# A convolution of 31 taps moved in part to TensorE: three channel groups as products of two taps each, one group on VectorE

## The chip, the cores and the metric

The kernel runs on one core of a Trainium2 chip. The metric is the device time of one execution in microseconds. TensorE multiplies matrices into PSUM, VectorE, ScalarE and GpSimd work on elements, SyncE issues most DMAs. Each engine takes its own instructions in order, and waits at the head of its queue when an operand is not ready.

## What is computed

Two layers of a streaming encoder on 256 tokens of 1024 channels: SwiGLU, mixer, SwiGLU in each, with RMS norms around. Layer 0 has the recurrent mixer that the change touches. Half of it is a delta-rule recurrence with 8 heads of 64 (computed here in four chunks of 64 tokens), the other half a causal convolution over 512 channels with 31 taps per channel, followed by a layer norm and SiLU:

```python
glu = c_val * jax.nn.sigmoid(c_gate)
conv = lax.conv_general_dilated(
    glu, conv_w[:, None, :], window_strides=(1,), padding=[(CONV_WIDTH - 1, 0)],
    dimension_numbers=('NWC', 'WIO', 'NWC'), feature_group_count=D_CONV) + conv_b
y_b = jax.nn.silu(layer_norm(conv, conv_ln_g, conv_ln_b, CONV_LN_EPS))
return jnp.concatenate([y_a, y_b], axis=-1) @ w_out
```

The layer norm needs all 512 channels of a token, and `w_out` needs both halves. All values are float32.

## The kernel before

Weights come as pages of 128 x 1024 floats (512 KB) into ten load buffers, in the order of use, on SP's queue. `Stream.page` then splits a page into a rounded part `whi` (ScalarE) and a rest `wlo` (VectorE, for some pages GpSimd), and a load can start when the page ten places earlier has been split. The large products use the two parts in three passes; the small products of the mixer take plain float32, which TensorE runs as two rows (two passes) each.

`mixer_a` calls its pieces in the order of `ORDER`; a scheduler then orders each engine's queue by a simulated timeline, so neighbouring pieces mix. The ones that matter here:

- `invert` (I) sends 64x64 matrices through memory and inverts their 16x16 blocks on VectorE; the results land in `G` and `T`.
- `glu` (C) makes the gated input of the convolution, channels on partitions in four groups of 128, tokens along the free axis.
- `conv` (c) sets the taps up. Groups 0 and 1 are VectorE's (60 taps, one multiply-add each, handed out by `feed`). Group 2 has 24 taps on TensorE, each a product with a diagonal matrix `dw` that ScalarE makes from the tap (handed out by `pfeed`), and six taps with group 3's thirty on ScalarE (multiply) and GpSimd (add).
- `amats` (A) makes the attention matrices `ak` and `ar` of the four chunks: TensorE products into two PSUM banks, four VectorE evictions per chunk. It hands out taps and products after each chunk.
- `doubling` (2) grows the inverses from 16 to 64: ten groups of 16 small products (`each`), 64x64 in one corner of the array, each group followed by a pair of convolution products, each evicted by VectorE (`WT`, `G`, `T`) and followed by taps.
- `convend` (n) adds up the rest and runs `conv_norm` for both token halves; `state` (S) is the recurrence over four chunks (`R,G`, then `vz`, `vz,kb`, `vz,ar`, `SB`), and `outproj` multiplies by `w_out`, convolution half first. The next SwiGLU follows.

The small products use four PSUM banks in turn (`abank`), group 2's sum one of the two `gu` banks.

## Time and profile before

| | us |
|---|---|
| median of three runs (1122.34 to 1145.09) | 1124.52 |
| profiled execution | 1123.03 |
| its span on the core | 1121.2 |
| mean granted TensorE clock | 0.983 |
| TensorE busy (share of the span) | 1075.6 (96%) |
| VectorE busy | 668.3 (60%) |
| ScalarE busy | 568.5 (51%) |
| GpSimd busy | 255.1 (23%) |

The profile is one execution, times in us from the start of the span. A matmul row's duration holds its way through the array, so the distance between the starts of neighbouring rows, not their duration, is what a row costs in a stream. Float32 products appear as two rows each. A name like `acc<-T,Q` is output and inputs, buffer numbers left out. The granted clock is given as a share of 2.4 GHz: 1.00 is 2.4 and 0.50 is 1.2 GHz, and values between are a mean over a stretch at either level.

### The profile page before, as it was taken

What the parts mean: (1) busy time and instruction counts of PE and PEld (TensorE: products, weight loads), DVE (VectorE), ACT (ScalarE), POOL (GpSimd) and SP (SyncE); (2) the same over time, 40 slices, a digit from 0 to 9 for tenths busy, and PEclk for the clock granted to TensorE, in tenths of its full rate; (3) what the DMA queues carried; (4) which work ended last, traced back from release to release, by engine and by line L of the source; (5) the groups of instructions that cost most, each with busy time, mean ns of one, the idle gap of its engine ahead of it and who ended that gap; (6) DMA issues with size and microseconds to landing.
All of it is one profiled execution on the core that took longest, in us unless ns stands there. A gap on an engine that the chain in (4) does not pass through costs nothing.

```text
span 1121.2 us, 17652 instructions
## 1 busy us (share of the span) xinstructions
PE 1075.6 (96%) x6955; PEld 947.1 (84%) x6955; DVE 668.3 (60%) x1064; ACT 568.5 (51%) x933; POOL 255.1 (23%) x194
## 2 busy tenths in 40 slices
PE   7999999999698899999989999999999989999997
PEld 5899998889587789999878999988887868999986
DVE  4465661599887556547444555836667665555722
ACT  7444553673453464446354544634666945444611
POOL 4200006571662170000070000001564540000000
PEclk9999999998798999999999999999999999999999
DMA  9766785245410246557554464744273553765400
GB/s 361 246 212 185 235 308 177 86 165 151 104 39 1 76 151 244 201 189 271 168 186 151 167 227 170 240 138 151 90 286 107 193 189 101 226 193 179 148 1 37
DMA packets 65321, 189.27 MB, mean 169 GB/s; under 512 B 18360, under 2 KB 19672, under 8 KB 65238
## 3 DMA queue, kind: packets, MB, share of 16 engines
q1 hardware_dynamic: 55386, 186.18, 49.4%
q10 hardware_dynamic: 9852, 1.96, 1.0%
q8 instruction: 54, 0.88, 0.3%
q14 instruction: 29, 0.24, 0.1%
HBM read 184.68 MB, written 2.92 MB: 167 GB/s over the span
## 4 chain that ended last, share of the span: by engine, by line
PE 66%; DVE 7%; ACT 2%; DMA 1%; issue 1%; POOL 1%; ACTq 0%; DVEq 0%; POOLq 0%
PE gu L352 23%; PE acc L263 16%; PE gu L223 12%; PE gu L338 5%; PE acc L370 3%; PE gu L585 2%; PE acc L585 2%; DVE cv L926 2%; DVE wlo L99 1%; DVE x L148 1%; PE tr L158 1%; POOL p L484 1%; PE tr L506 1%; ACT whi L98 0%; DMA raw<-in_cout_dram 0%
## 5 line engine op out<-in xcount | busy, mean ns | idle before, releaser
L98 ACT CAST whi<-raw 128x1024 fp32r<-128x1024 f32 x294 | 303.4, 1047 | 206.2 <-PE gu L352 110.8
L99 DVE TENSOR_TENSOR wlo<-raw,whi 128x1024 fp32r<-128x1024 f32 x248 | 312.5, 1266 | 133.9 <-ACT whi L98 108.1
L352 PE MATMUL gu<-xth,wlo 128*128 128x256 f32 x1104 | 314.1, 284 | 0.0
L352 PE MATMUL gu<-xl,whi 128*128 128x256 f32 x1104 | 313.1, 284 | 0.0
L352 PE MATMUL gu<-xth,whi 128*128 128x256 f32 x1104 | 313.1, 284 | 0.0
L352 PEld LDWEIGHTS gu<-xth,wlo 128*128 128x128 f32 x1104 | 212.0, 192 | 3.5 <-issue 0.9
L352 PEld LDWEIGHTS gu<-xth,whi 128*128 128x128 f32 x1104 | 211.8, 192 | 3.3 <-issue 0.7
L352 PEld LDWEIGHTS gu<-xl,whi 128*128 128x128 f32 x1104 | 211.9, 192 | 1.0 <-issue 0.8
L99 POOL TENSOR_TENSOR wlo<-raw,whi 128x1024 fp32r<-128x1024 f32 x46 | 113.9, 2506 | 300.1 <-PE gu L223 141.5
L263 PE MATMUL acc<-whi,ht 128*128 128x512 f32 x576 | 168.0, 393 | 0.0
L113 POOL TENSOR_TENSOR misc<-misc 128x1 f32<-128x1 f32 (+1 forms) x36 | 31.6, 880 | 476.0 <-DVE misc L130 380.7
L263 PEld LDWEIGHTS acc<-whi,ht 128*128 128x128 f32 x576 | 104.0, 189 | 18.3
L263 PE MATMUL acc<-wlo,ht 128*128 128x512 f32 x288 | 89.9, 392 | 0.0
L234 DVE TENSOR_TENSOR h<-gu,h 128x256 f32<-128x256 f32 x88 | 36.9, 420 | 77.9 <-ACT h L230 74.7
L232 DVE TENSOR_TENSOR h<-gu,misc 128x256 f32<-128x256 f32 x56 | 23.7, 424 | 80.1 <-PE gu L352 80.1
L223 PE MATMUL gu<-whi,xth 128*128 128x512 f32 x160 | 63.8, 403 | 1.8 <-ACT whi L98 1.8
L223 PE MATMUL gu<-wlo,xth 128*128 128x512 f32 x160 | 64.0, 400 | 0.5 <-DVE wlo L99 0.5
L263 PEld LDWEIGHTS acc<-wlo,ht 128*128 128x128 f32 x288 | 53.9, 188 | 11.8
L223 PE MATMUL gu<-whi,xl 128*128 128x512 f32 x160 | 63.3, 400 | 0.1
L233 ACT ACTIVATE h<-h 128x256 f32<-128x256 f32 x56 | 23.2, 415 | 53.7 <-DVE h L232 53.7
L230 ACT ACTIVATE h<-gu,misc 128x256 f32<-128x256 f32 x32 | 15.1, 475 | 66.9 <-PE gu L223 36.9
L338 PE MATMUL gu<-whi,xth 128*128 128x512 f32 x112 | 44.9, 401 | 1.1 <-ACT xth L162 0.9
(254 smaller groups left out, 1589.6 us busy)
## 6 DMA issues: line engine op xcount, KB each, us to landing
raw<-in_wgc_dram SPq DMA_DIRECT2D x112, 512.0 KB, 4.5
raw<-in_wd_dram SPq DMA_DIRECT2D x88, 512.0 KB, 4.7
raw<-in_wgt_dram SPq DMA_DIRECT2D x64, 512.0 KB, 5.3
raw<-in_cin_dram SPq DMA_DIRECT2D x24, 512.0 KB, 5.2
raw<-in_ain_dram SPq DMA_DIRECT2D x18, 512.0 KB, 4.5
raw<-in_aout_dram SPq DMA_DIRECT2D x8, 512.0 KB, 5.1
raw<-in_cgate_dram SPq DMA_DIRECT2D x8, 512.0 KB, 7.5
raw<-in_cout_dram SPq DMA_DIRECT2D x8, 512.0 KB, 3.7
```

The lines of the kernel that those rows point to most:

```text
L98: self.nc.scalar.copy(out=hi, in_=raw)
L99: (engine or self.nc.vector).tensor_tensor(out=lo, in0=raw, in1=hi.bitcast(F32), op=ALU.subtract)
L113: self.pow = self.nc.gpsimd.tensor_tensor(out=out, in0=v, in1=self.mhalf[:, :n], op=ALU.pow)
L223: nc.tensor.matmul(ps, lhsT=l, rhs=r[:, k % 2], start=n == 0, stop=n == 23)
L232: nc.vector.tensor_tensor(out=z, in0=ps[:, 0:256], in1=self.rb, op=ALU.mult)
L233: nc.scalar.activation(sl, z, AF.Silu)
L234: nc.vector.tensor_tensor(out=h, in0=ps[:, 256:512], in1=sl, op=ALU.mult)
L263: mm = nc.tensor.matmul(out, lhsT=l, rhs=r, start=u[1] == 0 and i + n == 0, stop=u[1] == NB - 1 and i * 3 + n == 5)
L338: self.nc.tensor.matmul(ps, lhsT=l, rhs=r[:, k % 2], start=n == 0, stop=n == 23)
L352: self.nc.tensor.matmul(ps[:, j * 256:(j + 1) * 256], lhsT=l, rhs=r, start=n == 0, stop=n == 23)
L370: self.nc.tensor.matmul(accs[t][c], lhsT=l, rhs=r[:, 0, c * 512:(c + 1) * 512], start=k == ks[0] and n == 0, stop=k == ks[7] and n == 2)
L585: return nc.tensor.matmul(out, lhsT=lhsT, rhs=rhs, start=start, stop=stop, skip_group_check=True)
```

## The change

Group 0 stays on VectorE (30 taps). Groups 1 to 3 go to TensorE as six blocks of 64 channels (`j` = 2 to 7), eight products each: the moving operand has 64 channels on one partition half and the same channels one token late on the other half (`gl[0]`, `gl[1]`; SP copies from half to half, four DMAs), so that a product with an offset of 2s tokens covers two taps. The columns of the weight make two sums, of which the second holds the taps that lie 16 tokens back; ScalarE takes the first sum with the bias into one partition half, VectorE copies the second, 16 tokens on, into the other, and a product with two stacked identities (`twice`) in `conv_norm` adds them as it transposes. The weights are six new pages `acw` that come ready from memory and are used from their load buffers without a split. The sums live in one of the four banks of `abank`, which has three while `busy`. The taps and products are handed out in other numbers (`FEED`, `PFEED`), the last 20 products behind `R,G` in chunks 0 and 1 of `state`, and `convend` now runs in chunk 1 behind its products. In `qmats`, `amats` and `each` the small products stand in another order: partition halves in turn, where before one half came whole.

```diff
-ORDER = "VLDKPQkRIBCcbA2nS"
+ORDER = "VLDKPQkRIBCcbA2S"
-CSPLIT, PTAPS = 6, 24
-FEED, PFEED = (4, 3, 12), (1, 2)
+FEED, PFEED = (3, 2, 6), (2, 2, 10)
...
             i, cols, _, pooled, early, whole = pg
             self.load(i + 1 + self.ahead)
             raw = self.tiles[i]
+            if whole:
+                pg[2] = raw.rearrange("p (k f) -> p k f", f=cols)
+                return pg[2]
...
+        def abank():
+            return self.abank(3 if m.get("busy") else 4)
...
         def qmats():
...
-                for hp in range(2):
+                for g in range(4):
                     for c in range(2):
-                        for g in range(4):
+                        for hp in range(2):
...
         def amats():
...
-                for hp in range(2):
-                    for g in range(4):
+                for g in range(4):
+                    for hp in range(2):
                         b = slice(64 * hp, 64 * hp + 64)
                         i = mm(pss[hp][:, g, :], both(bk, g, t, c)[b], both(ur, g, t, c)[b])
...
         def glu():
...
+            gl = m["glu"] = [grp(self.page("glu")) for _ in range(2)]
+            own, late = (slice(0, 64), slice(64, P)), (slice(64, P), slice(0, 64))
...
-                V.tensor_tensor(out=gl[:, 2 * h:2 * h + 2, :], in0=cv[:, 2 * h:2 * h + 2, :], in1=z, op=ALU.mult)
+                gs = slice(max(2 * h, 1), 2 * h + 2)
+                if h == 0:
+                    V.tensor_tensor(out=gl[0][:, 0, :], in0=cv[:, 0, :], in1=z[:, 0, :], op=ALU.mult)
+                for i, (o, l) in enumerate(zip(own, late)):
+                    m["gated"] = V.tensor_tensor(out=gl[i][o, gs, :], in0=cv[o, gs, :], in1=z[o, gs.start - 2 * h:2], op=ALU.mult)
+                    nc.sync.dma_start(out=gl[i][l, gs, 1:256], in_=gl[i][o, gs, 0:255])
...
             def each(t, lhsT, rhs):
...
-                for c in range(2):
-                    for h in range(8):
+                for h in range(8):
+                    for c in range(2):
                         cs = slice(64 * c, 64 * c + 64)
                         i = mm(ps[cs, h, :], lhsT(cs, h), rhs(cs, h))
                 pfeed(PFEED[1], i)
...
         def conv():
...
-                    elif g == 2 and 31 - CSPLIT - PTAPS <= d < 31 - CSPLIT:
-                            nc.scalar.activation(dw[:, i % 8, :], self.ident, AF.Copy, scale=w)
...
-                    elif g == 3 or g == 2 and d > 31 - CSPLIT:
-                        nc.scalar.activation(z, gl[:, g, 0:256 - d], AF.Copy, scale=w)
-                        nc.gpsimd.tensor_tensor(out=o, in0=z, in1=o, op=ALU.add)
...
+            W.upto(("acw",))
+            m["pconv"] = self.bank("acc11").rearrange("p (i t) -> p i t", t=256)
+            m["busy"] = True
+            m["ptaps"] = ((j, s, w[:, s, :]) for j, w in enumerate(W.get(("acw",)), 2) for s in range(8))
+            nc.gpsimd.memset(m["cval"][64:P, :, 0:16], 0.0)
+            nc.scalar.activation(m["cv"][0], m["glu"][0][:, 0, :], AF.Identity, scale=par("cw", 30), bias=par("cb0"))
+            m["taps"] = iter(range(1, 31))
...
         def pfeed(n, behind=None):
...
-                    mm(m["pconv"][:, d:256], w, m["glu"][:, 2, 0:256 - d], d == 31 - CSPLIT - PTAPS, d == 30 - CSPLIT)
+                    mm(o[:, 2 * s:256], w, m["glu"][j % 2][:, j // 2, 0:256 - 2 * s], s == 0, s == 7)
+                if s == 7:
+                    z = m["cv"][j]
+                    nc.scalar.activation(z[0:64], o[0:64], AF.Identity, bias=par("cb", j)[0:64])
+                    V.tensor_copy(out=z[64:P, 16:256], in_=o[64:P, 0:240])
...
         def conv_norm(t):
...
-            for g in range(4):
-                nc.tensor.transpose(out=tp[:, g * P:(g + 1) * P], in_=cv[:, g, t * P:(t + 1) * P], identity=self.ident)
+            nc.tensor.transpose(out=tp[:, 0:P], in_=m["cv"][0][:, ts], identity=self.ident)
+            for j in range(2, 8):
+                mm(tp[:, 64 * j:64 * j + 64], m["cv"][j][:, ts], self.twice)
...
         def state():
...
                 V.tensor_tensor(out=h8(vz[t][zs, c, :]), in0=pz[zs], in1=m["nn"][zs, t, :].unsqueeze(2).broadcast_to([64, 8, 64]), op=ALU.mult)
+                pfeed(PFEED[2], i)
...
+                if ch == 1:
+                    convend()
```

The first place is TensorE's queue at the start of the doubling. Before, `glu,dw` are group 2's products, `T,Q` the first groups, `vz,ak` part of chunk 0 of the recurrence:

```order
L585 MATMUL acc_3093<-ur,bk 128x128 x4
L585 MATMUL gu<-glu,dw 128x255
L585 MATMUL gu<-glu,dw 128x254
L585 MATMUL gu<-glu,dw 128x253
L585 MATMUL gu<-glu,dw 128x252
L585 MATMUL gu<-vz,ak 64x64 x8
L585 MATMUL acc_3112<-T,Q 64x64 x16
L585 MATMUL gu<-glu,dw 128x251
L585 MATMUL gu<-glu,dw 128x250
L585 MATMUL acc_3135<-T,Q 64x64 x16
L585 MATMUL gu<-glu,dw 128x249
L585 MATMUL gu<-glu,dw 128x248
```

And after, where `glu,raw` are the products of the six blocks (`raw` is the load buffer):

```order
L590 MATMUL acc_3061<-ur,bk 128x128 x4
L590 MATMUL gu<-vz,ak 64x64 x4
L590 MATMUL acc_3062<-ur,bk 128x128 x4
L590 MATMUL acc_2987<-glu,raw 128x244
L590 MATMUL acc_2987<-glu,raw 128x242
L590 MATMUL acc_3083<-T,Q 64x64 x16
L590 MATMUL acc_3105<-T,Q 64x64 x14
L590 MATMUL acc_2987<-glu,raw 128x256
L590 MATMUL acc_2987<-glu,raw 128x254
L590 MATMUL acc_3105<-T,Q 64x64 x2
L590 MATMUL acc_2987<-glu,raw 128x252
L590 MATMUL acc_2987<-glu,raw 128x250
```

The products ahead of the first group were four with made weights and are now eight with loaded ones, in pairs between the blocks of `amats`; four more stand behind the second group. The first group stands behind all of `amats` in both. Within a group the text of the rows is the same: the order of halves shows in the code alone.

The second place is VectorE's queue at the same time. `z` is the second half of the gate, `glu<-cv,z` the gate products, `ak` and `ar` the evictions of `amats`, `cv<-glu,cst,cv` the taps. Before:

```order
L773 COPY inv<-inv 128x256
L845 TENSOR_TENSOR z<-gu,misc 128x512
L847 TENSOR_TENSOR glu<-cv,z 128x512
L818 TENSOR_TENSOR ak<-acc_3035,cst 64x4x64
L821 TENSOR_TENSOR ar<-acc_3035,cst 128x4x64
L818 TENSOR_TENSOR ak<-acc_3036,cst 64x4x64
L821 TENSOR_TENSOR ar<-acc_3036,cst 128x4x64
L926 SCALAR_TENSOR_TENSOR cv<-glu,cst,cv 128x255 x2
L818 TENSOR_TENSOR ak<-acc_3054,cst 64x4x64
L821 TENSOR_TENSOR ar<-acc_3054,cst 128x4x64
L926 SCALAR_TENSOR_TENSOR cv<-glu,cst,cv 128x254 x2
L845 TENSOR_TENSOR z<-gu,misc 128x512
```

And after, where the taps are `glu<-glu,cst`:

```order
L866 TENSOR_TENSOR glu<-cv,z 64x256 x2
L778 COPY inv<-inv 128x256
L858 TENSOR_TENSOR z<-gu,misc 128x512
L823 TENSOR_TENSOR ak<-acc_3004,cst 64x4x64
L826 TENSOR_TENSOR ar<-acc_3004,cst 128x4x64
L823 TENSOR_TENSOR ak<-acc_3005,cst 64x4x64
L826 TENSOR_TENSOR ar<-acc_3005,cst 128x4x64
L930 SCALAR_TENSOR_TENSOR glu<-glu,cst 128x255
L866 TENSOR_TENSOR glu<-cv,z 64x512 x2
L823 TENSOR_TENSOR ak<-acc_3023,cst 64x4x64
L826 TENSOR_TENSOR ar<-acc_3023,cst 128x4x64
L930 SCALAR_TENSOR_TENSOR glu<-glu,cst 128x254
```

The second `z` stood behind four taps and six evictions, and now stands ahead of all; taps come singly.

The third place is SP's queue, with the copies from half to half (`glu<-glu`), the next stage's weights (`in_wgt`) and the inverses (`G`, `T`). Before:

```order
L69 DMA raw<-in_wgt_dram 128x1024
L740 DMA dq<-Q 64x8x64 x2
L69 DMA raw<-in_wgt_dram 128x1024 x4
L104 DMA gp<-in_gpost_dram 128x1024
L69 DMA raw<-in_wgt_dram 128x1024
L778 DMA G<-dg 64x8x64 x2
L778 DMA T<-dt 64x8x64 x2
```

And after:

```order
L106 DMA ln<-in_arow_dram 128x1024
L68 DMA raw<-in_acw_dram 128x1024 x3
L68 DMA raw<-in_wgt_dram 128x1024
L867 DMA glu<-glu 64x255 x2
L783 DMA G<-dg 64x8x64 x2
L783 DMA T<-dt 64x8x64 x2
L867 DMA glu<-glu 64x2x255 x2
L68 DMA raw<-in_wgt_dram 128x1024 x4
```

The first two copies stand behind one weight load of the next stage, the other two behind `G` and `T`; seven of the next stage's eight first pages are now behind them.

## Rows read from the trace of the kernel before

**Rows 1.** Busy time by stretch: length, TensorE, weight loads, VectorE, ScalarE, GpSimd, clock, DMA share, GB/s.

```profile
286.87:304.17 17.30, 6.52 (x65) 6.09 (x65) 14.29 (x23) 9.57 (x19) 12.76 (x7) 0.69 0.67 131
304.17:314.15 9.98, 9.94 (x96) 8.12 (x96) 5.60 (x16) 8.99 (x26) 4.04 (x7) 0.85 0.01 2
314.15:340.35 26.20, 23.80 (x304) 20.58 (x305) 25.27 (x42) 13.54 (x28) 19.16 (x28) 1.00 0.15 42
340.35:359.00 18.65, 16.95 (x184) 13.92 (x183) 14.06 (x31) 5.75 (x10) 3.75 (x5) 0.82 0.00 1
359.00:393.99 34.99, 32.11 (x192) 26.12 (x191) 19.83 (x35) 15.87 (x31) 5.62 (x5) 0.95 0.18 61
```

**Rows 2.** TensorE's timeline: start, duration, operation, rows; in brackets idle time and releaser.

```profile
304.17 3.45 PE L585 MATMUL gu<-glu,dw 128*128 128x255 f32 x8 [8.51 <-ACT dw L906]
...
314.89 1.90 PE L585 MATMUL acc<-G,WT 64*64 64x64 f32 x32 [0.78 <-DVE WT L866]
316.72 1.10 PE L585 MATMUL gu<-glu,dw 128*128 128x247 f32 x4
317.75 1.90 PE L585 MATMUL acc<-WT,G 64*64 64x64 f32 x32
319.57 1.09 PE L585 MATMUL gu<-glu,dw 128*128 128x245 f32 x4
```

**Rows 3.** VectorE's timeline: evictions, taps, gate.

```profile
292.29 2.65 DVE L926 SCALAR_TENSOR_TENSOR cv<-glu,cst,cv 128x255 f32<-128x255 f32 x2
294.97 0.43 DVE L818 TENSOR_TENSOR ak<-acc,cst 64x256 f32<-64x256 f32 x1
...
295.75 4.15 DVE L926 SCALAR_TENSOR_TENSOR cv<-glu,cst,cv 128x254 f32<-128x254 f32 x2
299.83 0.68 DVE L845 TENSOR_TENSOR z<-gu,misc 128x512 f32<-128x512 f32 x1
...
303.33 0.69 DVE L847 TENSOR_TENSOR glu<-cv,z 128x512 f32<-128x512 f32 x1
303.94 0.87 DVE L926 SCALAR_TENSOR_TENSOR cv<-glu,cst,cv 128x252 f32<-128x252 f32 x2
...
314.15 1.29 DVE L866 TENSOR_TENSOR WT<-acc,cst 128x512 f32<-128x512 f32 x2 [4.34 <-PE gu L585]
```

**Rows 4.** GpSimd's timeline at the same time.

```profile
290.44 2.81 POOL L99 TENSOR_TENSOR wlo<-raw,whi 128x1024 fp32r<-128x1024 f32 x1
293.21 1.45 POOL L889 TENSOR_TENSOR gg<-ln,gg 128x512 f32<-128x512 f32 x1
294.62 5.00 POOL L99 TENSOR_TENSOR wlo<-raw,whi 128x1024 fp32r<-128x1024 f32 x2
```

**Rows 5.** TensorE's timeline in chunk 1 of the recurrence.

```profile
352.20 0.69 PE L585 MATMUL acc<-vz,kb 128*64 128x64 f32 x16 [0.79 <-DVE vz L988]
352.72 1.10 PE L585 MATMUL gu<-vz,ar 128*64 128x64 f32 x16
353.75 0.66 PE L951 MATMUL tr<-cst,xc 128*128 128x128 f32 x4
```

**Rows 6.** TensorE's timeline behind the output product.

```profile
393.99 0.39 PE L223 MATMUL gu<-whi,xl 128*128 128x512 f32 x1
```

**Rows 7.** Busy time by stretch, two shorter ones, columns as in rows 1.

```profile
304.17:307.60 3.43, 3.43 (x9) 2.54 (x9) 3.38 (x10) 3.43 (x12) 0.00 (x0) 0.55 0.02 5
340.35:349.00 8.65, 7.96 (x66) 6.37 (x65) 8.03 (x18) 1.17 (x2) 1.03 (x2) 0.61 0.00 0
```

**Rows 8.** DMA issues of the stretch 200 to 300: queue, count, KB, us to landing.

```profile
prev<-pv ACTq DMA_DIRECT2D x2, 30.0 KB, 2.3
```

**Rows 9.** VectorE's timeline: first statistics and first split of the normalised half.

```profile
349.10 0.70 DVE L940 BATCH_NORM_STATS2 misc<-tr 128x6 f32<-128x512 f32 x1 [0.62 <-PE tr L938]
...
358.55 0.69 DVE L99 TENSOR_TENSOR xl<-yb,xth 128x512 fp32r<-128x512 f32 x1 [1.52 <-ACT xth L98]
```

More of the change, by code (lines that the diff above doesn't have):

```diff
@@ L53, in __init__, with add @@
         self.where, self.pages = {}, []
-    def add(self, key, ap, cols):
+    def add(self, key, ap, cols, whole=False):
         self.where.setdefault(key, [])
@@ L918, in conv @@
-            m["taps"], m["ptaps"] = iter(taps), iter(ptaps)
-            m["pconv"] = self.bank("gu", 2)[:, 0:256]
+            W.upto(("acw",))
+            m["pconv"] = self.bank("acc11").rearrange("p (i t) -> p i t", t=256)
+            m["busy"] = True
+            gl = m["glu"]
+            m["cv"] = [gl[1][:, 0, :], None] + [m["cval"][:, i, :] for i in range(4)] + [gl[i][:, 1, :] for i in range(2)]
+            m["ptaps"] = ((j, s, w[:, s, :]) for j, w in enumerate(W.get(("acw",)), 2) for s in range(8))
@@ L960, in convend @@
             pfeed(99)
-            for d, z in ((31 - CSPLIT - PTAPS, m["pconv"]), (31 - CSPLIT, m["part"])):
-                o = m["cv"][:, 2, d:256]
-                V.tensor_tensor(out=o, in0=z[:, d:256], in1=o, op=ALU.add)
+            m["busy"] = False
             for t in range(2):
@@ L970, in state @@
             ak, ar, kb, vz, ur, pc, G, Gg, Wg = (m[z] for z in ("ak", "ar", "kb", "vz", "ur", "pc", "G", "gg", "Wg"))
-            R = half(self.page("R"))
+            R = m["Q"].rearrange("p t h x -> p t (h x)")
             SB = self.temp("SB", [4, P])
@@ L1065, in plan @@
                     W.add(("ao", h // 2), flat(a["aout"][h]), 1024)
+                for j in range(6):
+                    W.add(("acw",), flat(a["acw"][j]), 128, True)
             if st == "C":
```

93 lines of the change are left out of this document (45 added, 48 removed).

## The prediction

> **What bounds the kernel now.** I read the page first for where the mixer lies, then the chain of waits for which engine holds it, then the busy time by stretch, then each engine's timeline there. The order of the built programs is the same on all engines outside the mixer and the first units of the stage behind it, so only 286.87 to 393.99 us is costed; the rest keeps its time.
>
> [rows 1] cuts that into five stretches. In the first (attention matrices, 17.30 us) TensorE works 6.52 us: it is not the bound. [rows 2] names its one long wait: 8.51 us until 304.17, for `dw`, the diagonal matrices that ScalarE makes of the taps, held behind the second gate. That gate's VectorE part `z` stands at 299.83, behind two taps of 4.15 us [rows 3]. In the third stretch (block doubling, 26.20 us) TensorE is busy 23.80 and VectorE 25.27: two bounds at once. There [rows 2] shows a steady beat: a group of 32 rows (16 products of 64x64, two rows each) takes 317.75 to 319.57 = 1.82 us, a pair of convolution products (four rows) 316.72 to 317.75 = 1.03. In the fourth TensorE has 1.70 us idle but a granted clock of 0.82, in the fifth 2.88 us idle.
>
> **Part 1, up to the first doubled block** (`WT`, 314.15 in [rows 3]). The wait for `dw` goes: the weights now come from memory, and the order puts both `z` ahead of all evictions. TensorE has there, ahead of the first group's end, its old 6.52 us [rows 1], eight products of 0.515 and blocks of some 2 us, 12.6 together, which fits. What sets the end is VectorE's queue, which has from 286.87 on: one `z` 0.68, two gate products of 0.69, 16 evictions of 0.43, 11 taps and one copy of about half a pair, 0.43 each [rows 3]. That is 0.68 + 1.38 + 6.88 + 5.2 = 14.1 us: the first `WT` at 301.0. This is the lower end. The upper end comes from GpSimd. [rows 4] shows it busy from 290.44 to 299.62, and [rows 3] what a tap costs then: the pair at 292.29 ends when the GpSimd rows of 290.44 and 293.21 have ended, the pair at 295.75 when both weight splits have, 2.65 and 4.15 us against 0.87 for the pair at 303.94. The evictions, which read a bank of PSUM, stay at 0.43. If each VectorE instruction with both inputs in SBUF costs one GpSimd row, then by 299.6 there have passed the gate products, the copy of the inverse, one tap and four evictions; 12 evictions, 10 taps and a copy remain, 5.2 + 4.3 + 0.4 = 9.9, and `WT` starts at 309.5. I take 307.0, near the hindered end, since both hindered pairs are two to five times the free one. Gain 7.1 (4.6 to 13.1).
>
> The Trainium skill, SBUF — State Buffer, "Who interferes with whom", says the same of the cause: a VectorE instruction with two SBUF inputs and a GpSimd instruction that reads SBUF take one port pair as a lock, and whoever starts second blocks. By that rule alone part 1 would end at the upper end (gain 4.6), by the free row at the lower (13.1). The trace agrees with the rule: 4.15 us for two taps under two splits.
>
> **Part 2, the doubling.** Behind the first `WT` stand eight groups and, in the new order, eight pairs (nine before). The pairs are as wide as before, 1.03. The groups' 32 rows are the same products, but neighbours now lie in opposite corners of the array instead of one. No row shows that order. Nearest: in [rows 5] `vz,kb`, whose outputs alternate between the partition halves, takes 352.20 to 352.72 for 16 rows, 32 ns each; `vz,ar`, same shape, always into one half, 352.72 to 353.75, 64 ns. At 32 ns a group takes 1.04. So 8 × 1.04 + 8 × 1.03 = 16.6, and the first wait for `WT` (314.15 to 314.89, [rows 2, 3]) plus a last short group, 1.1: 17.7 us against 26.20. Gain 8.5. If the new neighbours gain nothing it is 14.6 + 8.2 + 1.1 = 23.9, gain 2.3. VectorE must keep up: ten evictions of 0.69, 19 taps of 0.43 and two copies make 15.9, under 17.7 with GpSimd's additions gone. The last `G` comes at 324.7.
>
> **Part 3, the recurrence and the output product** (340.35 to 393.99, where the next stage's rows follow [rows 6]: 53.64 us before). It takes in 20 products that before did not exist. Four per mixer chunk stand where TensorE waited for VectorE, the others on the path: I count all, 20 × 0.515 = 10.3. The first chunk's `R,G` block, done ahead of 340.35 before, adds 0.9. The convolution's 14 transposing products for 8 add about 1.0. Given back: the clock. From 340.35 to 349.00 the granted clock was 0.61 [rows 7] while TensorE waited for the last taps and sums; at full clock its 7.96 busy us are 4.9, so 3.1 less. Also the 1.70 idle, and half of 2.88, which products fill: 3.1. Sum +10.3 + 0.9 + 1.0 − 3.1 − 3.1 = +6.0. Best case +3.5 (every gap filled, no extra for the transposes), worst +12.2 (nothing given back).
>
> **Costed at nothing.** ScalarE's diagonal matrices, the ScalarE and GpSimd chain of group 3: they leave; their engines wait for nothing that ends later. The copies one token late: 2.3 us to land by the like copy [rows 8], first needed behind chunk 0's blocks, where TensorE waits for VectorE anyway; without that cover 2.3 us. They stand in SP's queue behind one weight load that waits for a GpSimd split; 299.62 is the latest end of those [rows 4], the second pair of copies is needed behind the first groups, some 10 us later. The six weight pages hold six of the ten load buffers until the last product, about 18.6 us behind the last `G`, 343; the pages of the next stage that they delay are wanted at about 384, so 40 us cover. The bank taken from the four: chunks must wait for evictions one step earlier, inside VectorE's pace. The alternated rows of `amats` mostly fall back into groups of four in the built order, so I count no gain.
>
> **Sum.** −7.1 − 8.5 + 6.0 = −9.6 from the profiled execution's 1123.0 (span 1121.2 and 1.8 around): 1113.4, say 1113. That execution is 1.5 under the median of the runs, 1124.5.
>
> **Rivals.**
> - *Corners do not overlap.* The groups stay at 1.82. For it: a tap's neighbour is a product of the whole array, and each change between the two shapes may cost what overlap gives. Against: [rows 5]. Part 2 gains 2.3: 1119.6. The Trainium skill, TensorEngine Tiling (Array Packing), "Key Properties", speaks against this rival, since tiles load and multiply in parallel; no run here yet shows two corners in turn over a whole group.
> - *The ports are free enough.* GpSimd starts and ends its chain earlier and taps run at 0.43. Part 1 gains 13.1: 1107.4.
> - *The normalisation comes late.* It now starts when the last product has ended, and from the first statistics to the last split it took 349.10 to 359.24 [rows 9]. I have it covered by chunks 2 and 3, whose blocks are some 12 us. If it takes half as long again, TensorE is idle for 5 us ahead of the output product: 1118.4. For it: before, that product filled the gaps of chunks 2 and 3.
> - *The clock stays low: slower.* In [rows 7] eight rows of `dw` took 3.43 us at a granted 0.55, 0.42 each against 0.257 in the steady beat. TensorE idles much in part 1, as before, and the new groups are thinner work. If part 2 ran at the low level throughout, its 32 product rows cost 5.3 more and its groups 8.3 more: −9.6 + 13.6 = +4.0, 1127. It decides from about 70% of part 2 at the 1.2 GHz level. Against: the third stretch ran at 1.00 from its start [rows 1], and products fill it in the new order too.
>
> **How the numbers follow.** Forecast 0.55 (its own range 1106 to 1118, from the bounds of part 1 with 0.43 to 1.3 a tap and part 3 from +3.5 to +8), corners 0.15, free ports 0.12, late normalisation 0.10, low clock 0.08. The range 1105 to 1122 takes in all but the low clock and the far ends of part 3. Two per cent, about what a measurement can tell from no change, is 22 us here; only free ports with every best case come near it (−13.1 − 8.5 + 3.5 = −18.1), so faster by over 2% gets 0.03, slower 0.03, within 0.94.
>
> **What would show it.** Right: no wait for a weight ahead of the first group; 32 rows of a group in about 1.04 us; pairs at 1.03; first `WT` near 307, last `G` near 325, output product begun 30 us later, next stage at about 384; taps of 0.43 through the doubling. Wrong: groups at 1.82; TensorE waiting at a product for a copied half; a granted clock under 0.9 in the doubling; an output product that waits for the split of the normalised half.

## The result: 1% slower, outside the range

| | before | after |
|---|---|---|
| median of four runs, us | 1124.41 | 1135.33 (1134.39 to 1136.52) |
| ratio, 95% interval | | 1.0101 (1.0084 to 1.0119) |
| profiled execution, us | 1123.03 | 1136.52 |
| its span, us | 1121.2 | 1134.6 |
| mean granted clock | 0.983 | 0.978 |
| TensorE busy, us | 1075.6 | 1091.3 |
| VectorE busy, us | 668.3 | 662.3 |

The forecast was 1113.0 with a range of 1105 to 1122: 22 us too low, and the sign is wrong. Within two per cent, which had a chance of 0.94, came true, but a gain of 1% was meant and a loss of 1% came. Some executions, one of the four of before among them, keep a lower granted clock (0.96 in the mean over the span, not 0.98) and take some 20 us longer; the ratios leave them out, and three of the four of e14 below are of that kind.

Here and below, before and after are the two kernels' names. First the busy time of after by stretch (columns as in [rows 1]), cut at the first block, the first wide product, the first `WT`, the last `G` and the first row of the output product:

```profile
290.26:300.90 10.64, 2.11 (x21) 1.74 (x21) 10.44 (x16) 2.18 (x3) 7.36 (x5) 0.77 0.21 36
300.90:324.99 24.09, 24.09 (x123) 18.81 (x125) 13.42 (x27) 2.14 (x3) 4.67 (x5) 0.50 0.64 164
324.99:345.08 20.09, 20.09 (x329) 16.11 (x326) 14.93 (x30) 1.52 (x3) 0.11 (x1) 0.96 0.20 63
345.08:376.55 31.47, 29.11 (x300) 25.62 (x301) 13.04 (x24) 8.32 (x15) 2.20 (x2) 1.00 0.15 51
```

In the second row TensorE has no gap in 24 us, and all of it at the 1.2 GHz level. TensorE's timeline of after shows what it does there, and the steps behind it:

```profile
290.26 0.94 PE L590 MATMUL acc<-ur,bk 64*128 64x128 f32 x12
294.95 1.17 PE L590 MATMUL acc<-ur,bk 64*128 64x128 f32 x8 [3.75 <-DVE z L858]
300.90 2.04 PE L590 MATMUL acc<-glu,raw 128*128 128x256 f32 x4 [4.79 <-DVE ak L823]
...
321.05 1.99 PE L590 MATMUL acc<-glu,raw 128*128 128x244 f32 x4
322.97 3.47 PE L590 MATMUL acc<-T,Q 64*64 64x64 f32 x60
...
330.99 1.15 PE L590 MATMUL acc<-WT,G 64*64 64x64 f32 x32
332.07 1.09 PE L590 MATMUL acc<-glu,raw 128*128 128x244 f32 x4
...
346.30 1.14 PE L590 MATMUL acc<-Q,G 64*64 64x64 f32 x16
...
376.55 0.74 PE L372 MATMUL acc<-whi,xth 128*128 128x512 f32 x2 [1.23 <-ACT xth L100]
...
405.54 0.39 PE L225 MATMUL gu<-whi,xth 128*128 128x512 f32 x1
```

The wait for `dw` of [rows 2] is gone; in its place are two, 3.75 us for `z` and 4.79 us for the first evictions `ak`. The row at 300.90 also reads a copied half, and SP's timeline has the issue of the first copies:

```profile
298.28 1.17 SPq L867 DMA_DIRECT2D glu<-glu  x2
```

The first of them takes 2.5 us to land, so it is there at 300.8, within 0.1 us of the end of the third eviction (300.7). The profile names the eviction as what ended the wait; in e1 below the same product waits for the copy, and here the two came together. In sum the two waits are 8.54 us, no more than before had there: 8.51 for `dw` and 2.27 ahead of it. Before, too, came out of its wait at 1.2 GHz, but with eight wide rows in one piece, which lasted 3.43 us [rows 7]; behind them it had its full rate. In after a row of four wide ones takes 2.04 us behind the wait, against 1.09 at 332.07, and pairs and narrow blocks go on at the low level until the doubling. The next stage begins at 405.54 against 393.99 [rows 6], so 11.55 of the span's 13.4 us arise by the end of the mixer; the later stages take the other 1.9. VectorE's timeline of after, from the inversion of the blocks on:

```profile
284.50 3.42 DVE L773 TENSOR_TENSOR tmp<-inv 128x64 f32<-128x64 f32 x2
...
294.21 0.68 DVE L858 TENSOR_TENSOR z<-gu,misc 128x512 f32<-128x512 f32 x1
...
296.91 0.69 DVE L775 TENSOR_REDUCE inv<-tmp 128x64 f32<-128x512 f32 x1
...
297.85 0.86 DVE L866 TENSOR_TENSOR glu<-cv,z 64x256 f32<-64x256 f32 x2
...
299.04 0.69 DVE L858 TENSOR_TENSOR z<-gu,misc 128x512 f32<-128x512 f32 x1
299.64 0.41 DVE L823 TENSOR_TENSOR ak<-acc,cst 64x256 f32<-64x256 f32 x1
...
324.99 0.69 DVE L886 TENSOR_TENSOR WT<-acc,cst 128x512 f32<-128x512 f32 x1 [0.49 <-PE acc L590]
...
345.08 0.69 DVE L892 TENSOR_TENSOR G<-acc,G 128x512 f32<-128x512 f32 x1 [1.04 <-PE acc L590]
```

The last reduction of the inverse stands at 296.91. In the kernel before, VectorE's timeline has it 12.5 us earlier, and the step that takes 3.42 us above took 0.45:

```profile
277.61 0.45 DVE L768 TENSOR_TENSOR tmp<-inv 128x64 f32<-128x64 f32 x2
...
284.42 0.69 DVE L770 TENSOR_REDUCE inv<-tmp 128x64 f32<-128x512 f32 x1
```

Of the 12.5 us, 8.1 are a later start of the inversion (281.30 against 273.15) and the other 4.3 arise in it: the two instructions of 3.42 us end 0.1 us behind a weight split that GpSimd did from 285.37 to 287.80. So time was lost ahead of 286.87 too, in the part that the prediction left out. Its first trace on the chip is on GpSimd. In after, its timeline at the start and around 195 us:

```profile
1.14 0.25 POOL L849 MEMSET glu<- 64x3 f32 x2
...
192.82 4.72 POOL L101 TENSOR_TENSOR wlo<-raw,whi 128x1024 fp32r<-128x1024 f32 x2 [3.40 <-DMA lups<-in_alup_dram]
197.50 0.54 POOL L115 TENSOR_TENSOR misc<-misc 128x1 f32<-128x1 f32 x1
```

and of before:

```profile
177.72 14.20 POOL L99 TENSOR_TENSOR wlo<-raw,whi 128x1024 fp32r<-128x1024 f32 x6 [6.03 <-PE acc L263]
194.27 0.55 POOL L113 TENSOR_TENSOR misc<-misc 128x1 f32<-128x1 f32 x1 [2.35 <-DVE misc L130]
```

The first is the clearing of the two gated pages' first column (256 tokens need a zero ahead of the copy one token late). It names a VectorE instruction that it shall follow, yet GpSimd does it in the first 2 us, and the pages are in use from then on. From 148 us on the order differs: the vector `muv` is fetched at 185.89 (147.93 before), GpSimd's root of the norm at 197.50 stands behind two splits (194.27), the evictions of `Q` start at 269.13 (261.22).

### The profile page after: what moved, and what is told of

It reads as the page before. It is cut to its first block, busy times and chain, and to the rows that moved or that the text cites. A ratio compares the mean times of both kernels' runs of the same rounds, so it can differ in the third digit from the quotient of the medians.

```text
span 1134.6 us, 17690 instructions
## 1 busy us (share of the span) xinstructions
PE 1091.3 (96%) x7020; PEld 957.6 (84%) x7021; DVE 662.3 (58%) x1041; ACT 543.9 (48%) x876; POOL 230.2 (20%) x164
## 4 chain that ended last, share of the span: by engine, by line
PE 66%; DVE 3%; issue 3%; POOL 2%; ACT 1%; DMA 0%; POOLq 0%; DVEq 0%; SPq 0%; ACTq 0%
PE gu L354 23%; PE acc L265 16%; PE gu L225 11%; PE acc L590 5%; PE gu L340 5%; PE acc L372 1%; PE gu L590 1%; DVE x L150 1%; DVE tmp L773 1%; POOL p L486 1%; PE tr L160 1%; PE tr L508 1%; PE acc L495 0%; POOL misc L115 0%; PE tr L245 0%
## 5 line engine op out<-in xcount | busy, mean ns | idle before, releaser
L225 PE MATMUL gu<-whi,xth 128*128 128x512 f32 x160 | 63.5, 400 | 1.7 <-ACT whi L100 1.7
L100 ACT CAST fhi<-raw 128x1024 fp32r<-128x1024 f32 x40 | 41.3, 1046 | 10.4 <-DMA raw<-in_wgt_dram 8.6
```

Source lines behind the costliest of these rows:

```text
L100: self.nc.scalar.copy(out=hi, in_=raw)
L225: nc.tensor.matmul(ps, lhsT=l, rhs=r[:, k % 2], start=n == 0, stop=n == 23)
```

## The experiments

Three theories (the texts on record name theirs anew each time). **U, upstream**: the early clear makes another program from 148 us on; the inverse comes 12.5 us late and everything behind it. **C, clock**: what matters is TensorE's wait ahead of the first eviction; behind it the rows run at half the rate, and the loss is theirs whenever that wait comes. **P, port**: what makes the wait is VectorE's gate products under GpSimd's splits. Ratios are to the kernel before, run on the same chip beside it (medians 1124.1 to 1125.0).

### e1 and e2: the early clear

e1 is after with the clear behind a late GpSimd instruction (it then runs at 272.4):

```diff
-            nc.gpsimd.tensor_tensor(out=rk, in0=r, in1=k, op=ALU.mult)
+            m["rk"] = nc.gpsimd.tensor_tensor(out=rk, in0=r, in1=k, op=ALU.mult)
...
-                    with self.tc.issue_after(m["first"].ins):
+                    with self.tc.issue_after(m["rk"].ins):
                         nc.gpsimd.memset(gl[i][late[i], 1:4, 0:1], 0.0)
```

> The changed kernel with one edit: the clearing of the first column of the two gated pages (GpSimd) is queued behind GpSimd's product r x k late in the mixer. In the changed kernel nothing held it back, and it ran 1.14 us after the start, so the two pages were taken for the first 280 us of the kernel. Theory A (the two pages taken early push other tiles' places in SBUF about, and with them the whole order of the mixer ahead of the doubling): the order ahead of the attention matrices is that of before again, the block inversion on VectorE begins near 273 instead of 281.3 and its last reduction ends near 285 instead of 297.6, and the time falls by some 11 us, to 1124 (1120 to 1127). Theory B (the order ahead costs nothing, the loss comes from convolution products that TensorE does at the 1.2 GHz level between the attention matrices): the inversion still moves, but the first doubled block stays near 325 and the time stays at 1135.

e2 is before with two spare pages cleared at the start and once more late, so that they are held as long:

```diff
+            spare = [self.page("spare", bufs=2) for _ in range(2)]
+            for z in spare:
+                nc.gpsimd.memset(z[0:64, 0:3], 0.0)
...
+            with self.tc.issue_after(rkm.ins):
+                for z in spare:
+                    nc.gpsimd.memset(z[0:64, 0:3], 0.0)
```

> The kernel before with one addition: two spare pages, used for nothing, are cleared in three columns at the start and once more behind GpSimd's product r x k, so that they are taken over the same stretch as the two gated pages of the changed kernel. Theory A: the reordering alone costs what it costs in the changed kernel up to the end of the inversion, some 8 to 12 us: 1133 to 1136 against 1124.4. Theory B: 1124 to 1126, since nothing in the convolution is touched.

e2: 1144.53 us; its four executions took 1132, 1140, 1149 and 1150, ratio 1.0143 (1.0039 to 1.0247). It is slower than before, but by how much is not settled, and so neither is whether the 1133 to 1136 of its theory A hold. Its upstream is after's: `muv` at 186.84, `Q` at 270.43. VectorE's row of the inversion's start:

```profile
290.16 0.42 DVE L749 TENSOR_TENSOR inv<-inv,c 128x256 f32<-128x256 f32 x1 [7.47 <-DMA inv<-dq]
```

That is 17.0 us later than before's 273.15, 7.5 of them a wait for the matrices `dq` on their way through memory: two pages written early are enough to do it. e1 turns it round: `muv` at 149.27, the inversion at 275.26, its last reduction at 288.05, 8.9 us earlier than in after. And yet e1 takes 1137.77 us, ratio 1.0116 (1.0099 to 1.0132): nothing is won back, as its theory B has it. TensorE's row, two of VectorE's and GpSimd's, of e1:

```profile
299.61 2.04 PE L590 MATMUL acc<-glu,raw 128*128 128x256 f32 x4 [8.41 <-DMA glu<-glu]
```

```profile
294.25 5.04 DVE L866 TENSOR_TENSOR glu<-cv,z 64x256 f32<-64x256 f32 x2
299.33 0.69 DVE L858 TENSOR_TENSOR z<-gu,misc 128x512 f32<-128x512 f32 x1
```

```profile
294.01 5.00 POOL L101 TENSOR_TENSOR wlo<-raw,whi 128x1024 fp32r<-128x1024 f32 x2
```

The gate products now fall under two splits and take 5.04 us where they took 0.86 in after; the second `z` stands at 299.33, as late as in after (299.04), TensorE waits 8.41 us for the copied half (one of the prediction's signs of being wrong), and the slow stretch follows. So U is real, and taking it away alone wins nothing: the late inverse held evictions and copies in after, the slow gate products hold them in e1, to about the same moment.

### e3 and e4: the alternate order in the groups

e3 is before with the loops of `each` exchanged, and nothing else; e4 is after with them put back.

```diff
-                for c in range(2):
-                    for h in range(8):
+                for h in range(8):
+                    for c in range(2):
```

> The kernel before with one edit: in the doubling's groups the partition halves alternate from product to product (as in the changed kernel), nothing else. The order ahead of the doubling is that of before. If a group's 32 rows fall from 1.82 to 1.04 us here too, TensorE saves 10 x 0.78 = 7.8 us in the 26.2 us of the doubling; but VectorE was busy 25.27 of those. Theory A (VectorE binds there once TensorE is faster): 0 to 2 us gained, 1122.5 to 1124.5. Theory B (TensorE bound it): 6 to 8 us gained, 1117 to 1118.

> The changed kernel with one edit: the groups of the doubling go through one partition half whole, then the other, as before. Groups back at 1.82 us for 32 rows (1.08 now). VectorE has some 16 us of work in the 20.8 us of the doubling, so nothing hides it: eight groups on the path give +6 us, 1141 (1139 to 1143). If the evictions on VectorE set the pace instead: 1135 to 1137.

e3: **1119.45 us**, ratio 0.9958 (0.9943 to 0.9974), faster than both kernels by one exchange of two loops. TensorE's rows, a pair and a group: the next pair starts 1.08 us behind the group (317.81), where [rows 2] had 1.82, though VectorE has no gap left in the doubling (second fence, columns as in [rows 1]). The time lies between the forecasts of its theories, 1122.5 to 1124.5 and 1117 to 1118.

```profile
315.70 1.10 PE L585 MATMUL gu<-glu,dw 128*128 128x247 f32 x4
316.73 1.15 PE L585 MATMUL acc<-WT,G 64*64 64x64 f32 x32
```

```profile
314.00:338.68 24.68, 19.45 (x304) 15.77 (x305) 24.68 (x39) 14.07 (x29) 21.18 (x30) 0.93 0.15 45
```

That is not all that e3 gains: its last `G` stands at 338.68, only 0.9 us ahead of before's (339.62), while the last row of the output product starts 3.9 us ahead (389.63 against 393.54). The doubling takes 2.2 us less, behind a wait for `dw` that ends 1.3 later; the other 3.0 arise behind the last `G`, where before has a wait of TensorE of 2.10 us for VectorE's `x` (until 385.52) that e3 does not have. Why the exchange moves that was not tried.

e4: 1162.26 us, ratio 1.0334 (1.0248 to 1.0419). Its executions fall into two pairs, 1153.5 and 1154.5, and 1170.0 twice, where 1139 to 1143 was forecast. The profiled one is of the lower pair, and takes 18.0 us more than that of after (1154.54 against 1136.52); the upper pair has no trace. Ten groups at 0.74 us more (1.82 less 1.08) would be 7.4; the clock has the rest. By stretch, and one group and pair:

```profile
300.00:326.00 26.00, 25.51 (x124) 20.27 (x125) 14.01 (x29) 2.14 (x3) 5.16 (x5) 0.50 0.62 159
326.00:359.00 33.00, 33.00 (x294) 27.25 (x293) 14.30 (x29) 1.52 (x3) 0.11 (x1) 0.65 0.07 21
```

```profile
337.81 3.31 PE L590 MATMUL acc<-WT,G 64*64 64x64 f32 x32
341.05 1.99 PE L590 MATMUL acc<-glu,raw 128*128 128x244 f32 x4
```

With whole halves in the groups TensorE stays at 1.2 GHz until about 350; with alternate halves (after) it was back at 2.4 within the first two groups. In after the exchange is worth more than the time of its rows: the clock came back behind it.

### e5 and e8: wide work behind the wait

e5 is after with the eight early products together behind the last chunk of `amats`, as the eight rows of `dw` stood in before; e8 is after with 36 and 44 products of constants (bf16, 256 columns, result unused) behind chunks 0 and 1.

```diff
-                pfeed(PFEED[0], i)
+                pfeed(4 * PFEED[0] if ch == 3 else 0, i)
```

```diff
+                warm = self.bank("tr", 2) if ch < 2 else None
+                ones = self.ones.bitcast(BF16)
+                with self.tc.issue_after(i.ins):
+                    for _ in range((36, 44, 0, 0)[ch]):
+                        mm(warm[:, 0:256], ones[:, 0:P], ones)
```

> The changed kernel with one edit: the eight convolution products that stood in pairs behind the four chunks of the attention matrices stand together behind the fourth. TensorE's rows are the same. In the kernel before, TensorE came out of its long wait with eight wide rows in a row (the products with made weights, 3.45 us at 1.2 GHz) and ran at 2.4 GHz behind them; in the changed kernel it came out with four wide rows and narrow blocks between, and stayed at 1.2 GHz for 24 us. Theory A (the clock rises behind a run of wide rows and not behind pairs among narrow blocks): the 44 narrow rows and the first chunk's blocks take some 14 us at the low level, eight wide rows 4 us, eight at full 2, so the first doubled block comes near 320 instead of 325 and the time falls by 4 to 6 us to 1130 (1128 to 1132). Theory B (the low level comes from the waits, whatever the order): 325 and 1135.

> The changed kernel with filler on TensorE: 36 and 44 products of constants, 128 columns by 256, into a spare bank, behind the first two chunks of the attention matrices, about 0.11 us each at full clock, where TensorE waited 3.75 and 4.79 us for VectorE. They compute nothing that is used. Theory A (the work behind the waits is slow because the waits let the clock fall to 1.2 GHz): the stretch from 300.9 to 325 runs at 2.4 GHz in some 12 us, the first doubled block near 314, time 1125 (1122 to 1128). Theory B (the clock there is set by the narrow blocks themselves): the granted clock falls again behind the filler, the first doubled block at 322 or later, time 1133 or more.

e5: 1133.21 us, ratio 1.0086 (1.0066 to 1.0106). TensorE's timeline: the 16 rows at 315.09 begin at half rate and end at the full one, and the first groups run at full (60 rows in 1.97 us, against 3.47 in after).

```profile
315.09 4.95 PE L590 MATMUL acc<-glu,raw 128*128 128x256 f32 x16
319.96 1.97 PE L590 MATMUL acc<-T,Q 64*64 64x64 f32 x60
```

The granted clock was 0.50 from 300 to 315, 0.72 from 315 to 320, and 1.00 behind. So behind the wide rows in one piece it was back, behind pairs between narrow blocks it was not for 24 us. But they stand late here: the first `WT` comes at 321.52, 3.5 us ahead of after's, and the time, forecast at 1128 to 1132, is not told from after's (the intervals overlap). Here no product stands ahead of the rows that need the evictions, and TensorE waits for `ak` all the same, 11.38 us, until 301.36.

e8: 1134.45 us, ratio 1.0093 (1.0068 to 1.0118). The first filler ended at 293.1, and 8.77 us of waiting followed; the second ran behind the wait, from 305.85 to 311.44, on the path. By stretch:

```profile
305.85:311.40 5.55, 5.55 (x46) 4.70 (x45) 5.36 (x9) 0.00 (x0) 2.74 (x2) 0.85 1.17 242
311.40:321.20 9.80, 9.80 (x125) 7.98 (x123) 7.09 (x18) 0.47 (x1) 0.11 (x1) 1.00 0.40 138
```

Behind it the rest of the blocks and pairs took 311.44 to 319.34, 7.9 us; in after the like rows took 303.82 to 322.97, less the eight block rows (2.0) that e8 has ahead of the filler, some 17. Row by row, four wide ones take 1.10 us at 313.47 against 2.01 at 313.67 in after. That is C by itself: the same kind of rows in the same place, in about half the time. What it won, the filler's 5.6 us and the rows ahead of it ate: the time is not told from after's either.

### e6, e7 and e9: the upstream undone, and less ahead of the groups

e6 is e1 and e5 together. e7 is e1 with no products or taps ahead of the first group; e9 is e7 with `amats` called ahead of the gate.

```diff
-FEED, PFEED = (3, 2, 6), (2, 2, 10)
+FEED, PFEED = (0, 2, 6), (0, 3, 9)
```

```diff
-ORDER = "VLDKPQkRIBCcbA2S"
+ORDER = "VLDKPQkRIBACcb2S"
```

> The changed kernel with both edits: the two gated pages cleared late (order ahead of the doubling as before) and the eight products together behind the fourth chunk of the attention matrices. Alone, the late clear moved the inversion's end from 297.6 to 288.7 and the first doubled block by only 1.5 us, because TensorE's in-order queue stood 8.4 us at the first product, for the copies, until 299.6, and then did all blocks at 1.2 GHz. Theory A (that is what swallowed it): the blocks are done by 304, the products by 310, the first doubled block near 311 (308 to 314) instead of 323.5, time 1125 (1122 to 1128). Theory B (another limit there, VectorE's evictions and taps beside GpSimd): the first doubled block after 318, time over 1131.

> The changed kernel with the late clear and no convolution products among the attention matrices: three behind each of the ten groups of the doubling and nine in each of chunks 0 and 1 of the recurrence; taps 0, 2 and 6 behind attention chunks, WT and G where it was 3, 2, 6. Theory A: nothing on TensorE waits for the copies ahead of the doubling, the blocks end near 300 to 304, the first doubled block near 305, and the wide triples raise the clock there: last G near 333 instead of 343, time 1127 (1123 to 1130). Theory B (without wide rows ahead of it the doubling starts at 1.2 GHz and stays there for ten us or more): last G after 340, time 1135 or more.

> The kernel of the run without early products (late clear, three products behind each group), with one more edit: the attention matrices are called ahead of the gated input, so that TensorE makes them while the weights' products of the gate still run and VectorE evicts them ahead of the gate. In that run VectorE's two gate products took 5.04 us under two GpSimd weight splits (293.04 to 298.12) with all evictions behind them; TensorE waited 9.14 us for the first one, until 299.28, and did the rest of the blocks at 1.2 GHz until 312.98. Theory A (the evictions' place behind both gates is what holds TensorE and lets its clock fall): no narrow block is left behind 300, the first doubled block comes when the inverses are back from memory, at 303 to 309 instead of 315, and the time is 1122 (1118 to 1125). Theory B (the doubling then starts at 1.2 GHz, with narrow groups and no wide rows ahead, and stays there): the gain is given back, last G at 337 or later, time 1128.

e6: 1132.84 us, 1.0082 (1.0064 to 1.0099). e7: 1128.91, 1.0047 (1.0029 to 1.0064). Both show the slow gate products again (e6: the gate products take 5.04 us at 293.20, under two splits of 5.00 from 292.95), and TensorE waits for `ak`, 8.87 us until 299.43 and 9.14 until 299.28, at 0.50 behind. In e7 eight wide products fewer stand ahead of the first `WT`, which is at 315.05, against 320.06 in e6; the 305 that was forecast it misses, with a time inside the range (1123 to 1130). e9 has TensorE done with the matrices by 282: 1127.84, 1.0021 (1.0010 to 1.0033). The wait moved, and so did the place where the gate products fall under splits. GpSimd, VectorE and TensorE of e9:

```profile
297.83 9.76 POOL L101 TENSOR_TENSOR wlo<-raw,whi 128x1024 fp32r<-128x1024 f32 x4 [10.13 <-ACT whi L100]
```

```profile
302.82 5.05 DVE L866 TENSOR_TENSOR glu<-cv,z 64x256 f32<-64x256 f32 x2
```

```profile
301.99 2.08 PE L590 MATMUL acc<-T,Q 64*64 64x64 f32 x62 [1.30 <-DMA T<-dt]
311.48 1.97 PE L590 MATMUL acc<-G,WT 64*64 64x64 f32 x32 [7.41 <-DVE WT L886]
```

The first groups run at full rate by 304, and then wait 7.41 us for a `WT` (310.73) that stands behind the gate products. Behind the wait the next group takes 1.97 us, at the low level again (0.50 from 311.48 to 313.45).

### e10, e11 and e12: the splits away from GpSimd

All three give the splits of the `ao0` weights to VectorE: e10 is e7 with it, e11 before with it alone, e12 is e9 with it.

```diff
-POOLED = ("ak", "alora", "ao0", "ar", "av", "d0", "d1", "g1", "gate0")
+POOLED = ("ak", "alora", "ar", "av", "d0", "d1", "g1", "gate0")
```

> The kernel of the run without early products, with one more edit: the first two pages of the output product's weights are split by VectorE instead of GpSimd, so that GpSimd is idle from about 293 on. Theory A (the gate products take 5.04 us because GpSimd's splits hold the port that both need): the pair takes 0.9 us; VectorE has the splits itself, 1.2 us each, so the evictions begin only 1 to 3 us earlier and the time is 1127 (1124 to 1129). Theory B (the pair is slow for itself): 5 us again, and with the added splits the time is 1131 or more.

> The kernel before with one edit: the first two pages of the output product's weights are split by VectorE instead of GpSimd. Theory A (port): the two pairs of taps of 2.65 and 4.15 us become 0.9 us each, 5 us saved on VectorE ahead of the second gate, against 1.2 us for each split that lands in the same stretch: the wait for the made weights ends 0 to 4 us earlier and the time is 1122 (1120 to 1125). Theory B: the taps stay at 2 us or more each, time 1126 to 1130.

> Both of the last edits together on the kernel without early products: attention matrices ahead of the gated input, and the output product's first pages split by VectorE. If both theories A hold, the gates are quick and nothing is queued behind them: first doubled block at 303 to 308 and copies landed by 300, time 1120 (1116 to 1124). If the splits on VectorE now stand ahead of what the doubling waits for, it is no better than with the matrices ahead alone.

e10: 1127.78 us, 1.0031 (1.0020 to 1.0043). The cause of the slow gate products is shown: the same two take 0.86 us, with GpSimd idle. What they cost is not shown by it, for VectorE's own splits now stand ahead of `z`, which comes at 298.00 (298.12 in e7), and the time is not told from e7's:

```profile
294.02 0.86 DVE L866 TENSOR_TENSOR glu<-cv,z 64x256 f32<-64x256 f32 x2
294.91 1.23 DVE L101 TENSOR_TENSOR wlo<-raw,whi 128x1024 fp32r<-128x1024 f32 x1
```

e11: 1133.35, 1.0080 (1.0065 to 1.0095), slower: by itself the move makes VectorE (no gap from 313.26 to 345) later in the doubling, and the clock falls to 0.60 from 330 on. Neither of its theories (1120 to 1125, 1126 to 1130) has that.

e12: 1123.69 us (1119.69 to 1125.17, ten runs), ratio 0.9989 (0.9977 to 1.0002), inside its forecast of 1116 to 1124 and not told from before. Against e9 that is 4.2 us by the one move of the splits, and the first `WT` stands 5.3 us earlier. By stretch, cut at its first `WT`, last `G` and first output product row:

```profile
290.00:305.45 15.45, 11.74 (x142) 11.26 (x141) 12.08 (x15) 7.97 (x9) 0.00 (x0) 1.00 0.86 203
305.45:329.52 24.07, 22.40 (x334) 19.15 (x335) 19.14 (x40) 1.99 (x4) 0.36 (x3) 1.00 0.56 183
329.52:360.33 30.81, 28.64 (x293) 24.61 (x293) 14.97 (x29) 7.80 (x15) 2.20 (x2) 1.00 0.16 52
```

With the early clear, the evictions' place behind the gate and the splits beside it all away, the clock is 1.00 in these three stretches (0.74 in the 20 us ahead, 0.94 in the 28 behind), TensorE waits for nothing over 3.4 us, the first `WT` comes at 305.45, and the next stage begins at 388.67, 5.3 us ahead of before. The 305.45 cannot be set against the forecast of 307.0 as it stands: the eight early products, 4.1 us at the full rate, stand behind `WT` here, and the doubling with three products a group takes 24.07 us where after takes 20.09. Against after the median is 11.6 us lower; 10.9 had been lost. The gain at the mixer's end does not last: from the last row of the output product to the end the span has 731.2 us, before 727.7, after 729.5, e3 726.9. Why the later stages of this build take 3.5 us more was not tried.

### e13 and e14: the other alternate orders

The change alternates halves in `qmats` and `amats` too, which the prediction counted as no gain. e13 is before with all three places alternated, e14 with these two alone.

```diff
-                for hp in range(2):
-                    for g in range(4):
+                for g in range(4):
+                    for hp in range(2):
```

> The kernel before with the alternate order of halves in all three places of the change: the attention matrices, the inverse's starting matrices and the groups of the doubling. Theory A (the alternation pays only where TensorE sets the pace, that is in the groups; the attention matrices wait for VectorE's evictions in either order): as with the groups alone, 1119.5 within 1.5. Theory B (the narrow blocks too are worth something, four columns' pairs side by side): the blocks of eight rows take under 1.2 us instead of 2 and the time is 1117 or less. Theory C (the alternation of the attention matrices makes both banks of a chunk come free and full at the same time, so evictions start later): 1121 to 1125.

> The kernel before with alternate halves in the attention matrices and the inverse's starting matrices, and the groups of the doubling as before. Theory A (alternation pays only in the groups): 1124.4 within 1.5, groups at 1.82. Theory B: faster by 2 or more. Theory C (evictions of a chunk start later because both banks fill together): slower by 1 to 5, first block of the doubling later than 314.2.

e13: **1118.78 us** (1117.96 to 1119.20), ratio 0.9948 (0.9929 to 0.9967), the fastest of all kernels, but not to be told from e3: the groups carry it, as theory A has it. e14 settles nothing on its price: its four executions took 1121.01, 1140.08, 1145.16 and 1146.68 us, too far apart for a ratio, and no theory on record has the upper three. The profiled one is that of 1145.16, and what it shows is told as an observation of that execution alone. Its busy time by stretch, and then that of e13:

```profile
300.00:315.00 15.00, 15.00 (x88) 12.19 (x85) 13.87 (x27) 8.04 (x21) 7.05 (x8) 0.50 0.12 36
315.00:345.00 30.00, 29.22 (x213) 24.57 (x212) 12.35 (x24) 8.30 (x18) 10.66 (x17) 0.50 0.01 1
345.00:370.00 25.00, 25.00 (x182) 20.97 (x181) 16.10 (x32) 5.38 (x12) 8.32 (x13) 0.50 0.14 43
```

```profile
298.50:313.71 15.21, 15.21 (x92) 12.22 (x92) 15.03 (x30) 8.54 (x25) 5.98 (x7) 0.50 0.13 36
313.71:339.69 25.98, 20.41 (x342) 16.32 (x341) 23.91 (x41) 14.06 (x29) 21.02 (x30) 1.00 0.13 43
```

Both wait some 10 us for the evictions (until 298.64 and 298.50) and go on at the low level with blocks and products in turn. With alternate groups (e13) the clock is back by 313.71; with whole halves (e14, this execution) TensorE works without a gap of 1 us and stays at 0.50 for 70 us. e4 and after differ in the same way. Why e14 took 1121 once, and whether the whole halves alone make the other three, was not seen in a trace and stays open.

## Why the prediction was wrong, point by point

| step | forecast | measured |
|---|---|---|
| the program ahead of 286.87 | unchanged | inverse done 12.5 us later |
| first `WT` | 307.0 | 324.99 (e12, no products ahead of it: 305.45) |
| from there to the last `G` | 17.7 | 20.1 |
| a group of 32 rows / a pair | 1.04 / 1.03 | 1.08 / 1.02 |
| part 3, to the next stage | 59.6 | 59.2 (346.30, the first row that needs the last `G`, to 405.54) |
| next stage begins | 384.4 | 405.54 |
| behind the mixer | 0 | +1.9 |

From the forecast to the profiled execution these are 23 us: 18.0 up to the first `WT`, 2.4 from there to the last `G`, 0.7 from there to the next stage, 1.9 behind it. The last was not traced to a cause.

**The first step that failed** is "The order of the built programs is the same on all engines outside the mixer and the first units of the stage behind it, so only 286.87 to 393.99 us is costed; the rest keeps its time." The clear's place in GpSimd's queue, ahead of everything, was to be read in the built program and was not, and the order does differ from 148 us on. e1 and e2 show the effect on the inverse, in both directions: early clearing of two pages does it. By what way, the room that the pages take in the on-chip memory or another, no run shows.

**The second is Part 1**, and it decides. "The order puts both `z` ahead of all evictions" was read as the end of a wait. It is a wait: TensorE had the blocks to do that its free banks take (20 rows) and then nothing until the first `ak` and the first copied half, which now stood behind the gate products, the `ak` behind the second `z` as well, and all of them behind the inverse. The term "12.6 together, which fits" was near as work: 2.11 us ahead of 300.90, and 24.09 at 0.50, which are 12.0 at full clock. But 12.0 of these 14.2 ran behind the wait instead of beside it, and at half the rate. So of the 18.0 us by which `WT` missed 307.0, 12.0 are clock (24.09 less 12.0) and 6.0 the late start (the 12.0 of work from 300.90 on end at 312.9). This split is an estimate. e8 shows the first directly: the like rows in about half the time. e12 shows that with the wait away both go.

The upper end of Part 1 (309.5) counted one GpSimd row for each VectorE instruction with both inputs in SBUF, the gate products too. That price was right, 5.04 us for two under two splits against 0.86 without (e6, e10). In after itself the gate products took 0.86, and it was the inversion that stood under GpSimd's rows. The Trainium skill, SBUF — State Buffer, "Who interferes with whom", states that a VectorE instruction with two SBUF inputs and a GpSimd instruction that reads SBUF contend for one port pair as for a lock; the traces agree: 5.04 us of VectorE under 5.00 of GpSimd. What the sum left out is what TensorE pays for waiting behind them.

**Part 2 held in its prices.** The corners overlap: 1.08 against 1.82, also in e3. The Trainium skill, TensorEngine Tiling (Array Packing), "Key Properties", states that different tiles can load and multiply in parallel; the trace agrees, and the rival against it is out. Of the 2.4 us too few, one is a ninth pair and most of the rest the first rows, still at half rate. **Part 3 held in its sum**: 59.2. But the late normalisation, one of the rivals, shows in part: TensorE waits 1.23 us for its `xth` at the first row of the output product and 1.68 at 387.67, 2.9 together where the rival had 5. Of what was costed at nothing, the copies had no cover in e1 (8.41 us ended by `glu<-glu`) and cost 0.93 us in e12; in after the first landed within 0.1 us of the evictions that TensorE needed next.

**The low clock** was a rival with a chance of 0.08, put in the doubling, with a price of 13.6. It came one step earlier, in Part 1, at 12.0, and together with the 6.0 of the late start it made the sign. Its argument against, "products fill it in the new order too", is what failed: pairs between narrow blocks filled every gap and the clock stayed at 0.50.

**Where the gain went.** Put right, the convolution on TensorE starts the last row of the output product at 388.2 (e12), and the alternation alone at 389.6 (e3; before 393.5). Of the 8.5 us that Part 2 forecast, 6.2 were to come from the exchanged loops, which need no convolution on TensorE. The move with all its troubles away is 1.4 us ahead of them at the mixer's end and 4.2 behind at the kernel's (1123.69 against 1119.45).

## What to carry to other kernels

Cost a wait of TensorE with the work behind it: 8.5 us of waiting ahead of pairs and narrow blocks cost some 12 us more than the wait itself, where a wait as long ahead of eight wide rows cost some 1.4 (before: 3.43 us for the eight at first, 0.257 each in the steady beat). Here it was cheaper to remove what TensorE waits for (e12) than to fill behind it (e8). Read the whole built order of each engine, the first microseconds too: a small clear at 1.14 us shifted work from 148 us on. Try the small side edits of a change alone: here an exchange of two loops gave the only gain over before that was measured.

## What was not expected of the hardware

- Without a gap and without full rate: behind 8.5 us of waiting TensorE was busy 24.09 of 24.09 us at 1.2 GHz (after). What it did before the clock rose: eight wide rows in a piece (before), 16 (e5), 44 wide bf16 rows (e8), groups in alternate corners (after, e13). With whole halves in the groups it stayed low from the first group at 322.55 to about 350, without a gap (e4).
- Two gate products on 64 partitions took 0.86 us with GpSimd idle (e10) and 5.04 under two of its splits (5.00), ending 0.3 us behind them (e1).
